# VectorE alone forms the Strassen-Winograd combinations of activations, and the second batch is transposed into two pairs of banks in turn

## The chip, the core and the metric

The kernel runs on one core of a Trainium2 chip. The time is the device time of one execution in microseconds (us), median of three runs; lower is better. TensorE multiplies 128x128 blocks and writes its results into PSUM, which has eight banks of 128 partitions x 512 fp32 elements. VectorE, ScalarE and GpSimd do the elementwise work; SyncE issues most DMAs. In the profile they are PE, DVE, ACT, POOL and SP, and PEld is TensorE's loading of weights.

## The reference

One encoder layer is applied to two batches of 512 tokens with the same weights. Only its beginning matters for the change: the normalised activations h and the wide input projection.

```python
def rms_norm(x, g):
    xf = x.astype(jnp.float32)
    y = xf * lax.rsqrt(jnp.mean(xf * xf, axis=-1, keepdims=True) + EPS) * g.astype(jnp.float32)
    return y.astype(x.dtype)

def hybrid_layer(x, norm_g, w_in, ...):
    h = rms_norm(x, norm_g)                       # (1, 512, 1024)
    proj = jnp.einsum('bsd,de->bse', h, w_in)     # w_in: 1024 x 6848
    c_q, c_kv, k_rope, gate_a, conv_in, gate_c, mg_a, mg_c = split_columns(proj)
    ...                                           # attention, convolution, merge
    u = conv_in[..., :CONV_WIDTH] * jax.nn.sigmoid(conv_in[..., CONV_WIDTH:])
    ...                                           # width-31 depthwise convolution of u, and the rest

y_prompt = hybrid_layer(x_prompt, ...)
y_sample = hybrid_layer(x_sample, ...)
```

## The kernel before

**Precision.** Every fp32 operand of a matmul is held as two rounded parts, a high part H and a low part L = value - H, and a product is three matmuls: H·H, L·H and H·L. For a weight block `i`, `split` makes `whi` (ScalarE, L128) and `wlo` (L129, VectorE for the first four blocks, GpSimd later).

**The two batches.** Batch 0 (prompt) and batch 1 (sample) have 512 tokens each, in four tiles `xt` of 128 tokens. `norm_x` squares and sums a tile on ScalarE (L263), forms the factor `rr` on VectorE and GpSimd (L264, L251) and scales the tile on VectorE (L267, L270). `trans_x` transposes it on TensorE into PSUM tiles `xT` (L275), one tile of one bank for each block k of 128 channels, k from 0 to 7. `evac_x` writes the high part `hH` (ScalarE, L306) and the low part `hL` (VectorE, L307).

**Combinations.** A part of the projection (`seven`, from about 113 us on) computes four 512-wide products with seven, after Strassen and Winograd, treating the two batches and the two halves of the channels as a 2x2 block matrix. It needs four combinations of the activations for each k from 0 to 3, each with a high and a low part, `tH` and `tL`. `whole_x` first adds `hH` and `hL` of batch 0 to `xw` on GpSimd (L284). Then `combine_x(k)` works on the banks of batch 1 for k and k + 4:

- `b22` is bank k + 4 times the gain (ScalarE, L290);
- `t1 = bank k * gain - xw[k]` and `t3 = bank k * gain - b22` (VectorE, L291 and L292);
- `t2 = b22 - t1` and `t4 = xw[k+4] - t2` (GpSimd, L293 and L294);
- for each of t1, t3, t2, t4, `tH` is a rounded copy (ScalarE, L298) and `tL = t - tH` (GpSimd, L299).

The buffers of t1 to t4 and of `b22` are single, so the next k waits until they are read.

**Banks.** At the beginning pool `pp` holds three pairs of banks and pool `p1` two single banks. Two of the pairs hold `first[0]` and `first[1]` (named `blk`), the first two projection blocks. Batch 1 is transposed into the two single banks of `p1`, for k and k + 4 together; the transposes of the next k wait until all readers of these two banks are done: `hH`, `hL`, `b22`, t1 and t3. The third pair of `pp` is free during this time.

**From the preparation to the steady part.** `block_mm` for batch 0 of the two blocks (48 matmuls) runs while batch 1 is normalised; 48 more follow for batch 1. Then both pools are closed, and six single banks `pb` take the place of `pp`. The first block after that (`pbi`, `single`) is given the two banks of `first[1]`. It may start when those have been read: ScalarE makes `sig`, the sigmoid of `first[0]` (L487, after a load of its table), and VectorE multiplies `first[1]` by it into `u` (L494), in two halves. The weights `whi` and `wlo` have three buffers each, so those of the fourth block (`split` ahead of `sig` on ScalarE and ahead of `u` on VectorE) wait until the matmuls of `first[0]` have read the first block's.

**What sets the order.** The whole program is written down in one pass; a list scheduler then places each engine's instructions in an order of its own, from dependencies and priorities, except inside the `manual_schedule` blocks. So an edit at the beginning may move instructions elsewhere as well. At run time each engine takes its instructions strictly in that order.

Of the kernel before, what the change touches and what calls it, by code (L numbers as in the profile page):

```python
# [9 lines left out]
F32 = mybir.dt.float32  # L10
# [7 lines left out]
P = 128  # L18
D = 1024
S = 512  # L20
# [23 lines left out]
def encoder_block(tc, xp_d, xs_d, win_d, wkr_d, whd_d, wqr_d, wo_d, wp_d, wout_d, vec_d, dwk_d, rg_d, rc_d, yp_d, ys_d):  # L44
    nc = tc.nc
    opened = {}

    def open_pool(name, **kw):
        if kw.get("space") is not DRAM:
            kw["reuse_waits"] = "tile"  # L50
        cm = tc.tile_pool(name=name, **kw)
        opened[name] = cm
        return cm.__enter__()
# [5 lines left out]
    f = lambda ap: ap.bitcast(F32)  # L59
    mm = nc.tensor.matmul  # L60
    ACT = nc.scalar.activation
    DVE = nc.vector
# [17 lines left out]
    pp = open_pool("pp", bufs=3, space=PSUM)  # L80
# [191 lines left out]
    def trans_x(b, banks, ks):  # L272
        for tt in range(4):
            for k in ks:
                nc.tensor.transpose(banks[k][:, tt * P : (tt + 1) * P], xt[4 * b + tt][:, k * P : (k + 1) * P], identf)  # L275

    tp = open_pool("hT", bufs=1, side="right")
    TH = {(n, k): tp.tile([P, S], F32R, name=f"tH{n}_{k}") for n in (1, 2, 3) for k in range(4)}
    TL = {(n, k): tp.tile([P, S], F32R, name=f"tL{n}_{k}") for n in (1, 2, 3) for k in range(4)}
    xw = {k: tp.tile([P, S], F32, tag=f"t4_{k}", name=f"xw{k}") for k in range(KD)}  # L280

    def whole_x(k):

        nc.gpsimd.tensor_add(xw[k], f(hH[k, 0]), f(hL[k, 0]))  # L284

    def combine_x(k, banks):
        g1, g2 = (vec[:, V_NG + q : V_NG + q + 1] for q in (k, k + 4))
        b22 = xpool.tile([P, S], F32, tag="b22", name=f"b22_{k}")
        t = {n: wp.tile([P, S], F32, tag=f"s{n}", bufs=1, name=f"t{n}_{k}") for n in (1, 2, 3, 4)}
        ACT(b22, banks[k + 4], AF.Identity, scale=g2)  # L290
        DVE.scalar_tensor_tensor(t[1], banks[k], g1, xw[k], op0=ALU.mult, op1=ALU.subtract)  # L291
        DVE.scalar_tensor_tensor(t[3], banks[k], g1, b22, op0=ALU.mult, op1=ALU.subtract)  # L292
        nc.gpsimd.tensor_sub(t[2], b22, t[1])  # L293
        nc.gpsimd.tensor_sub(t[4], xw[k + 4], t[2])  # L294
        TH[4, k] = tp.tile([P, S], F32R, tag=f"t4_{k}", name=f"tH4_{k}")
        TL[4, k] = tp.tile([P, S], F32R, tag=f"t4_{k + 4}", name=f"tL4_{k}")
        for n in (1, 3, 2, 4):
            nc.scalar.copy(TH[n, k], t[n])  # L298
            nc.gpsimd.tensor_sub(TL[n, k], t[n], f(TH[n, k]))  # L299

    def evac_x(b, banks, ks):
        for k in ks:
            g = vec[:, V_NG + k : V_NG + k + 1]
            hi = hp.tile([P, S], F32R, name=f"hH{k}_{b}")
            lo = hp.tile([P, S], F32R, name=f"hL{k}_{b}")
            ACT(hi, banks[k], AF.Identity, scale=g)  # L306
            DVE.scalar_tensor_tensor(lo, banks[k], g, f(hi), op0=ALU.mult, op1=ALU.subtract)  # L307
            hH[k, b], hL[k, b] = hi, lo

    def x_bank(b, k):  # L310
        return p1.tile([P, S], F32, tag="p1", name=f"xT{b}_{k}")
# [121 lines left out]
    banks = {}  # L433
# [18 lines left out]
        block_mm(first[i], i, hh, hl, (0,))  # L452
    for k in range(KD):
        whole_x(k)
    for k in range(4):
        banks = {kk: x_bank(1, kk) for kk in (k, k + 4)}
        trans_x(1, banks, banks)
        evac_x(1, banks, banks)
        combine_x(k, banks)
    for i in (0, 1):  # L460
        block_mm(first[i], i, hh, hl, (1,))
        ensure(3 + i)
# [119 lines left out]
    pp = open_pool("pp", bufs=3, space=PSUM)  # L582
# [373 lines left out]
    for s_ in range(4 * NU + 3):  # L956
        n, j = divmod(s_, 4)
# [46 lines left out]
    pp = open_pool("pp2", bufs=4, space=PSUM)  # L1004
# [131 lines left out]
```

## Time and profile before

| | us |
|---|---|
| time, median of 3 runs (lowest to highest) | 1182.81 (1182.19 to 1184.61) |
| the profiled execution: its time, its span | 1184.55, 1182.8 |
| TensorE busy | 1145.4 (97%) |
| VectorE, ScalarE, GpSimd busy | 763.1, 488.5, 343.3 |
| granted TensorE clock, mean | 0.99 |

The profile shows one execution. The span is the time from its first to its last instruction; the execution took 1.75 us more than its span. A row of a timeline has the start in us, the duration in us, the engine, the line, the operation, and in brackets the idle time before it with what ended it. A row of the chain has start, duration, engine, name and line. A row of the waits has who waited for whom, then the sum in us, the number of times, and the longest. A row of the windows has the stretch, its length, then busy time and count for PE, PEld, DVE, ACT and POOL, and last the granted clock (1.00 is full speed), the DMA share and GB/s.

### The profile page before, as it was taken

What the parts mean: (1) busy time and instruction counts of PE and PEld (TensorE: products, weight loads), DVE (VectorE), ACT (ScalarE), POOL (GpSimd) and SP (SyncE); (2) the same over time, 40 slices, a digit from 0 to 9 for tenths busy, and PEclk for the clock granted to TensorE, in tenths of its full rate; (3) what the DMA queues carried; (4) which work ended last, traced back from release to release, by engine and by line L of the source; (5) the groups of instructions that cost most, each with busy time, mean ns of one, the idle gap of its engine ahead of it and who ended that gap; (6) DMA issues with size and microseconds to landing.
All of it is one profiled execution on the core that took longest, in us unless ns stands there. A gap on an engine that the chain in (4) does not pass through costs nothing.

```text
span 1182.8 us, 15035 instructions
## 1 busy us (share of the span) xinstructions
PE 1145.4 (97%) x5856; PEld 969.4 (82%) x5856; DVE 763.1 (65%) x1112; ACT 488.5 (41%) x909; POOL 343.3 (29%) x292
## 2 busy tenths in 40 slices
PE   6689999999999999999999999999999999999998
PEld 4468888888888888877888887899999998888887
DVE  5589899989999962652212454787877789344311
ACT  6522344343343222871101335776676687122200
POOL 5853566586576322200000001322122221000000
PEclk9889999999999999999999999999999999999999
DMA  6011223223223444534343012101100111344431
GB/s 253 1 54 71 71 89 111 86 71 107 89 107 107 160 147 151 158 115 160 138 142 125 23 52 76 39 26 34 35 25 19 36 36 37 107 135 166 161 107 72
DMA packets 46519, 109.52 MB, mean 93 GB/s; under 512 B 3696, under 2 KB 20336, under 8 KB 46448
## 3 DMA queue, kind: packets, MB, share of 16 engines
q1 hardware_dynamic: 41552, 91.78, 23.6%
q10 hardware_dynamic: 4896, 16.78, 3.5%
q8 instruction: 46, 0.75, 0.3%
q14 instruction: 25, 0.20, 0.1%
HBM read 79.18 MB, written 29.36 MB: 92 GB/s over the span
## 4 chain that ended last, share of the span: by engine, by line
PE 92%; POOL 3%; ACT 3%; DVE 1%; issue 1%; DMA 1%; SPq 0%; ACTq 0%; DVEq 0%
PE blk L325 22%; PE pbi L325 20%; PE po L1058 7%; PE pt L825 2%; PE pbd L356 2%; PE pba L356 2%; PE pbb L356 2%; PE pbd L358 2%; PE pba L358 2%; PE pbb L358 2%; PE pbb L357 2%; PE pbd L357 2%; PE pba L357 2%; PE pkv L733 1%; PE pkv L735 1%; PE pkv L734 1%
## 5 line engine op out<-in xcount | busy, mean ns | idle before, releaser
L412 DVE SCALAR_TENSOR_TENSOR py<-u,dwk,py 128x1024 f32<-128x1024 f32 x224 | 288.5, 1288 | 6.2
L128 ACT CAST whi<-raw 128x1024 fp32r<-128x1024 f32 (+3 forms) x59 | 60.5, 1025 | 282.0 <-PE blk L325 165.8
L325 PE MATMUL pbi<-hH,whi 128*128 128x512 f32 x352 | 138.9, 395 | 8.1 <-DVE u L494 8.1
L325 PE MATMUL pbi<-hL,whi 128*128 128x512 f32 x352 | 137.9, 392 | 0.0
L325 PE MATMUL pbi<-hH,wlo 128*128 128x512 f32 x352 | 108.9, 391 | 0.0
L129 DVE TENSOR_TENSOR wlo<-raw,whi 128x1024 fp32r<-128x1024 f32 (+2 forms) x38 | 53.4, 1405 | 59.9 <-ACT whi L128 59.9
L325 PEld LDWEIGHTS pbi<-hH,whi 128*128 128x128 f32 x352 | 66.6, 189 | 22.1 <-DVE u L494 8.5
L325 PEld LDWEIGHTS pbi<-hH,wlo 128*128 128x128 f32 x352 | 66.5, 189 | 14.0
L325 PEld LDWEIGHTS pbi<-hL,whi 128*128 128x128 f32 x352 | 66.7, 190 | 13.6
L179 POOL TENSOR_TENSOR olo<-s,ohi 128x512 fp32r<-128x512 f32 x44 | 57.5, 1318 | 52.7 <-ACT ohi L178 52.7
L129 POOL TENSOR_TENSOR wlo<-raw,whi 128x1024 fp32r<-128x1024 f32 x20 | 48.4, 2418 | 83.5 <-ACT whi L128 83.5
L325 PE MATMUL blk<-a,whi 128*128 128x512 f32 x256 | 68.4, 389 | 0.0
L816 ACT ACTIVATE pr<-sc,nm,sqs 128x512 f32<-128x512 f32 x64 | 51.2, 800 | 28.3 <-DVE nm L814 28.2
L251 POOL TENSOR_TENSOR rk<-sk,mhalf 128x4 f32<-128x4 f32 x16 | 17.2, 1074 | 147.7 <-DVE sk L743 147.7
L325 PE MATMUL blk<-hH,whi 128*128 128x512 f32 x144 | 57.6, 406 | 1.2 <-ACT hH L306 0.7
L325 PE MATMUL blk<-hL,whi 128*128 128x512 f32 x144 | 57.8, 401 | 0.5 <-DVE hL L307 0.4
L178 ACT CAST ohi<-s 128x512 fp32r<-128x512 f32 x44 | 26.2, 620 | 75.2 <-PE pbi L325 51.0
L325 PEld LDWEIGHTS blk<-a,whi 128*128 128x128 f32 x256 | 48.0, 188 | 9.9
L179 POOL TENSOR_TENSOR olo<-raw,ohi 128x512 fp32r<-128x512 f32 x33 | 43.7, 1324 | 35.2 <-ACT ohi L178 26.5
L325 PE MATMUL blk<-cH,whi 128*128 128x512 f32 x128 | 50.7, 396 | 2.4 <-ACT whi L128 2.4
L1061 DVE TENSOR_TENSOR o<-po,xr 128x1024 f32<-128x1024 f32 (+1 forms) x9 | 10.0, 1106 | 64.2 <-PE po L1058 64.2
L603 DVE TENSOR_TENSOR tmc<-blk,smc 128x1024 f32<-128x1024 f32 x8 | 9.8, 1225 | 64.2 <-PE blk L325 64.2
(272 smaller groups left out, 3076.5 us busy)
## 6 DMA issues: line engine op xcount, KB each, us to landing
raw<-in_win_dram SPq DMA_DIRECT2D x53, 512.0 KB, 3.6
y_s<-y SPq DMA_DIRECT2D x8, 512.0 KB, 4.0
ga_s<-stga ACTq DMA_DIRECT2D x8, 512.0 KB, 2.6
gc_s<-stgc ACTq DMA_DIRECT2D x8, 512.0 KB, 2.6
yt<-y_s SPq DMA_DIRECT2D x8, 512.0 KB, 5.3
gt<-gc_s SPq DMA_DIRECT2D x8, 512.0 KB, 4.1
mc_s<-stmc ACTq DMA_DIRECT2D x8, 512.0 KB, 3.4
raw<-in_wp_dram SPq DMA_DIRECT2D x8, 512.0 KB, 5.1
```

The source lines that it names most:

```text
L128: nc.scalar.copy(hv, rv)
L129: (sub or DVE).tensor_sub(lv, rv, f(hv))
L178: nc.scalar.copy(hi[:, sl], src)
L179: nc.gpsimd.tensor_sub(lo[:, sl], src, f(hi[:, sl]))
L325: mm(ps[b] if isinstance(ps, list) else ps[:, b], (wlo if wl_ else whi)[:, k], xl(k, b) if xl_ else xh(k, b), start=(k == 0 and wl_ == 0 a ...
L356: mm(ps, hi[:, k], xh, start=first and k == 0, stop=False, skip_group_check=not first)
L357: mm(ps, hi[:, k], xl, start=False, stop=False, skip_group_check=not first)
L358: mm(ps, lo[:, k], xh, start=False, stop=k == 3, skip_group_check=not first)
L412: DVE.scalar_tensor_tensor(out, u[:, :, i : i + S], dwk[:, j, i : i + 1], src, op0=ALU.mult, op1=ALU.add)
L816: ACT(pr, ps, AF.Exp, bias=nm, scale=r["sq"][:, j : j + 1], accum_out=sm)
L825: nc.tensor.transpose(pt[:, kt], pr[:, kt * P : (kt + 1) * P], identf)
L1058: mm(ps[:, n], lhs[k][:, ts_], w[k][:, n * S : (n + 1) * S], start=first_, stop=last_)
```

## The change

The four kinds of subtraction that GpSimd did in `combine_x` (t2, t4 and the four `tL` of each k: 24 in all) are given to VectorE. And batch 1 is transposed into two pairs of banks in turn: k = 0 and 2 use the single banks of `p1` as before, k = 1 and 3 use the third pair of `pp`. `combine_x(k)` is written after the transposes and evacuation of k + 1. Seven lines are added, so that lines after 461 have a number that is 7 higher afterwards: `u` is L501 and `sig` is L494 there.

```diff
@@ combine_x
         ACT(b22, banks[k + 4], AF.Identity, scale=g2)
         DVE.scalar_tensor_tensor(t[1], banks[k], g1, xw[k], op0=ALU.mult, op1=ALU.subtract)
         DVE.scalar_tensor_tensor(t[3], banks[k], g1, b22, op0=ALU.mult, op1=ALU.subtract)
-        nc.gpsimd.tensor_sub(t[2], b22, t[1])
-        nc.gpsimd.tensor_sub(t[4], xw[k + 4], t[2])
+        DVE.tensor_sub(t[2], b22, t[1])
+        DVE.tensor_sub(t[4], xw[k + 4], t[2])
...
         for n in (1, 3, 2, 4):
             nc.scalar.copy(TH[n, k], t[n])
-            nc.gpsimd.tensor_sub(TL[n, k], t[n], f(TH[n, k]))
+            DVE.tensor_sub(TL[n, k], t[n], f(TH[n, k]))
@@ encoder_block
     for k in range(KD):
         whole_x(k)
-    for k in range(4):
-        banks = {kk: x_bank(1, kk) for kk in (k, k + 4)}
-        trans_x(1, banks, banks)
-        evac_x(1, banks, banks)
-        combine_x(k, banks)
+    held = {}
+    for k in range(5):
+        if k < 4:
+            if k % 2:
+                two = pp.tile([P, 2, S], F32, tag="pp", name=f"xT1_{k}")
+                held[k] = {k: two[:, 0], k + 4: two[:, 1]}
+            else:
+                held[k] = {kk: x_bank(1, kk) for kk in (k, k + 4)}
+            trans_x(1, held[k], held[k])
+            evac_x(1, held[k], held[k])
+        if k > 0:
+            combine_x(k - 1, held[k - 1])
```

What the scheduler makes of it is seen at three places. In the names the first number is k (or, for `t` and `tL`, the k of the combination), and the last one numbers the buffer.

The first place is VectorE at the end of the preparation, up to `u`. Its reading of `blk_312`, which is `first[1]`, frees two banks for `pbi`. Before:

```order
L307 SCALAR_TENSOR_TENSOR hL_1_470<-xT_3_459,vec,hH_1_469 128x512
L307 SCALAR_TENSOR_TENSOR hL_1_474<-xT_7_460,vec,hH_1_473 128x512
L291 SCALAR_TENSOR_TENSOR t_3_478<-xT_3_459,vec,xw_151 128x512
L292 SCALAR_TENSOR_TENSOR t_3_480<-xT_3_459,vec,b_3_477 128x512
L129 TENSOR_TENSOR wlo_555<-raw_552,whi_554 128x1024
L494 TENSOR_TENSOR u_583<-blk_312,sig_580 128x512 x2
L412 SCALAR_TENSOR_TENSOR py_651<-u_583,dwk,y_649 128x1024
```

And now:

```order
L307 SCALAR_TENSOR_TENSOR hL_1_452<-xT_3_438,vec,hH_1_451 128x512
L294 TENSOR_TENSOR t_2_459<-xw_154,t_2_457 128x512
L299 TENSOR_TENSOR tL_2_142<-t_2_457,tH_2_130 128x512
L291 SCALAR_TENSOR_TENSOR t_3_476<-xT_3_438,vec,xw_151 128x512
L292 SCALAR_TENSOR_TENSOR t_3_478<-xT_3_438,vec,b_3_475 128x512
L299 TENSOR_TENSOR tL_2_466<-t_2_459,tH_2_465 128x512
L293 TENSOR_TENSOR t_3_477<-b_3_475,t_3_476 128x512
L299 TENSOR_TENSOR tL_3_139<-t_3_476,tH_3_127 128x512
L299 TENSOR_TENSOR tL_3_147<-t_3_478,tH_3_135 128x512
L294 TENSOR_TENSOR t_3_479<-xw_155,t_3_477 128x512
L299 TENSOR_TENSOR tL_3_143<-t_3_477,tH_3_131 128x512
L129 TENSOR_TENSOR wlo_553<-raw_550,whi_552 128x1024
```

Behind these rows stand `u`, twice, and then the last `tL`. All but one of the 24 subtractions stand ahead of `u` on VectorE.

The second place is ScalarE at the same point of the program. Before:

```order
L298 CAST tH_3_135<-t_3_480 128x512
L128 CAST whi_554<-raw_552 128x1024
L128 CAST whi_592<-raw_590 128x1024
L298 CAST tH_2_449<-t_2_443 128x512
L298 CAST tH_3_131<-t_3_479 128x512
L487 ACT_TABLE_LOAD
L487 ACTIVATE sig_580<-blk_287 128x512 x2
```

And now:

```order
L298 CAST tH_3_135<-t_3_478 128x512
L298 CAST tH_3_131<-t_3_477 128x512
L128 CAST whi_552<-raw_550 128x1024
L494 ACT_TABLE_LOAD
L494 ACTIVATE sig_578<-blk_287 128x512 x2
L128 CAST whi_590<-raw_588 128x1024
L298 CAST tH_3_485<-t_3_479 128x512
```

The copy of the fifth block's weights (`whi_590`) and the copy of a t4 now stand behind `sig`, not ahead of it.

The third place is TensorE in the attention, far from the edit, where head 0 of batch 1 and the preparation of head 1 are interleaved (`sc` are scores, `pkr` transposed keys). Before:

```order
L787 MATMUL pkT_0_5838<-identf,ks_0_5749 128x128 x4
L794 MATMUL pkr_0_5847<-identr,kk_0_5729 128x128 x4
L809 MATMUL sc_1_2_5813<-k_1_5628,qrT_1_5572 128x512
L810 MATMUL sc_1_2_5813<-k_1_5629,qrT_1_5572 128x512
L796 MATMUL pkr_0_5848<-identr,kk_0_5729 128x128 x4
L835 MATMUL av_0_1_5861<-pt_5769,vh_0_5295 128x256
```

And now:

```order
L794 MATMUL pkT_0_5836<-identf,ks_0_5747 128x128 x4
L816 MATMUL sc_1_2_5811<-k_1_5626,qrT_1_5570 128x512
L817 MATMUL sc_1_2_5811<-k_1_5627,qrT_1_5570 128x512
L801 MATMUL pkr_0_5845<-identr,kk_0_5727 128x128 x4
L803 MATMUL pkr_0_5846<-identr,kk_0_5727 128x128 x4
L842 MATMUL av_0_1_5859<-pt_5767,vh_0_5293 128x256
```

Two matmuls of the scores moved ahead of four transposes. Elsewhere after the beginning TensorE's order is unchanged; on VectorE some steps of the convolution (L412) change places with their neighbours by one or a few, ScalarE and GpSimd have a few such exchanges, and SyncE has one.

## The prediction

> **What bounds the kernel now.** I read the page first (part 1, then the chain that ended last), then TensorE's waits, the chain in order of time at the beginning, and the timeline there.
>
> ```profile
> PE 1145.4 (97%) x5856; PEld 969.4 (82%) x5856; DVE 763.1 (65%) x1112; ACT 488.5 (41%) x909; POOL 343.3 (29%) x292
> PE 92%; POOL 3%; ACT 3%; DVE 1%; issue 1%; DMA 1%; SPq 0%; ACTq 0%; DVEq 0%
> PE pbi L325 <- DVE u L494: 8.1, 1, 8.1
> PE xT L275 <- ACT b L290: 4.6, 3, 2.5
> PE pkr L796 <- ACT k L798: 1.9, 1, 1.9
> ```
>
> TensorE is the bound, and a change elsewhere pays only where TensorE waits. Its longest wait after the start is one of 8.1 us, of the first block `pbi` for `u`; the next, 4.6 us in three parts, is of the second batch's transposes for `b22`. The change is aimed at both. In the attention no wait is longer than 1.9 us. The chain shows what stands behind the first two:
>
> ```profile
> 32.00 0.75 DVE hL L307
> 34.14 1.27 POOL tL L299
> 42.95 1.23 POOL t L293
> 47.56 7.87 PE blk L325 x24
> 55.45 1.06 ACT whi L128
> 56.84 5.28 issue
> 63.55 1.29 DVE u L494 x2
> 64.88 7.27 PE pbi L325 x22
> ```
>
> From 34 us on the chain goes through GpSimd, then TensorE, then 5.28 us that it cannot explain ("issue"). The timeline does:
>
> ```profile
> 55.45 2.18 ACT L128 CAST whi<-raw 128x1024 fp32r<-128x1024 f32 x2 [1.21 <-PE blk L325]
> 56.54 7.09 DVE L129 TENSOR_TENSOR wlo<-raw,whi 128x1024 fp32r<-128x1024 f32 x1 [2.96 <-ACT whi L128]
> 59.06 0.62 ACT L298 CAST tH<-t 128x512 fp32r<-128x512 f32 x1 [0.91 <-POOL t L293]
> 59.70 1.28 ACT L487 ACT_TABLE_LOAD   x1
> 60.99 1.09 ACT L487 ACTIVATE sig<-blk 128x512 f32<-128x512 f32 x2
> 64.88 0.80 PE L325 MATMUL pbi<-hH,whi 128*128 128x512 f32 x1 [8.11 <-DVE u L494]
> 533.50 1.22 DVE L129 TENSOR_TENSOR wlo<-raw,whi 128x1024 fp32r<-128x1024 f32 x1 [4.58 <-ACT whi L128]
> 34.14:66.00 31.86, 18.73 (x69) 12.97 (x70) 17.86 (x16) 19.41 (x30) 31.77 (x30) 0.78 0.03 10
> ```
>
> Two things delay `u`. ScalarE's queue waits for GpSimd's `t` (0.91 us, ahead of the table and `sig`, which ends at 62.08). And VectorE's `wlo`, which takes 1.22 us at 533.50, takes 7.09 us here, to 63.6, while GpSimd is busy without a gap: 31.77 of the 31.86 us from 34.14 on (last row, fifth pair). So `sig` alone would have let `u` begin at 62.1; the slow `wlo` costs 1.4 us more.
>
> [...]
>
> **The new list on VectorE.** GpSimd loses 24 subtractions, VectorE gains them; 23 stand ahead of `u`. With GpSimd out of the way the list can be priced from undisturbed rows.
>
> ```profile
> 32.67 0.74 DVE L291 SCALAR_TENSOR_TENSOR t<-xT,vec,xw 128x512 f32<-128x512 f32 x1
> 33.33 0.74 DVE L307 SCALAR_TENSOR_TENSOR hL<-xT,vec,hH 128x512 fp32r<-128x512 f32 x1
> 658.50 1.89 DVE L645 TENSOR_TENSOR kvL<-kvn,kvH 128x512 fp32r<-128x512 f32 x3
> 662.10 0.68 DVE L645 TENSOR_TENSOR kvL<-kvn,kvH 128x512 fp32r<-128x512 f32 x1
> L298 ACT CAST tH<-t 128x512 fp32r<-128x512 f32 x15 | 9.0, 616 | 7.7 <-POOL t L293 6.1 <-DVE t L291 0.9 <-DVE t L292 0.7
> ```
>
> Three-operand instructions follow each other 0.67 us apart (32.00, 32.67, 33.33). A subtraction of the kind of `tL` takes 0.68 alone and three take 1.89, so they stand 0.605 apart; `wlo` then takes about 1.14 from its neighbour. From the first `hL` of batch 1 at 32.00 to `u` the order has 16 of the first (8 `hL`, 4 t1, 4 t3), 23 of the second and one `wlo`: 10.7 + 13.9 + 1.1 = 25.7, so `u` could start at 57.7. Its two halves take 1.29: `pbi` could start at 59.0. ScalarE has 15 casts of 0.62 where it had 15 before and keeps up.
>
> - ScalarE's chain to `sig`: the t2 of k = 3 is the 35th in the list (16 three-operand ones, 19 subtractions), done at 32.0 + 22.2 + 0.1 = 54.3; its cast to 54.9; `whi` 1.06, the table 1.28, `sig` 1.09: 58.3. The second half of `u` then ends at 59.0 as well. Both lists meet.
> - TensorE can be later. `whi` needs the buffer of the first block's weights, so nearly all of `first[0]` and `first[1]`. The `hL` of k = 3 is the 24th in VectorE's list (13 and 11), done at 47.4; 28 matmuls remain, 6.4 us at the 0.227 us spacing below: 53.8, hidden under 54.9. At half clock they take longer, by 1.7 us (one 3.4 us stretch) to 3.4 us (two): 55.5 to 57.2. `whi` starts some 0.5 before the last, so between 54.9 and 56.7, and `pbi` 4.1 us later (1.06 + 1.28 + 1.09 + 0.68).
>
> So `pbi` starts between 59.0 and 60.9. I take 60.2, near the upper end, since the next rows show the clock at half speed in just this part. Against 64.88 that is 4.7 us earlier (4.0 to 5.9).
>
> ```profile
> 38.45:41.85 3.40, 2.09 (x11) 1.25 (x12) 1.50 (x2) 2.65 (x5) 3.40 (x4) 1.00 0.01 2
> 41.85:45.25 3.40, 1.09 (x4) 0.55 (x4) 1.50 (x2) 1.19 (x3) 3.40 (x3) 1.00 0.00 0
> 45.25:48.65 3.40, 3.06 (x11) 2.24 (x12) 1.51 (x3) 2.98 (x6) 3.40 (x4) 0.50 0.01 2
> 48.65:52.05 3.40, 3.40 (x10) 2.63 (x9) 1.19 (x2) 0.46 (x1) 3.40 (x4) 0.50 0.00 0
> 52.05:55.45 3.40, 3.40 (x16) 2.80 (x15) 1.05 (x2) 1.88 (x4) 3.40 (x4) 1.00 0.00 0
> 55.45:58.85 3.40, 1.32 (x6) 0.75 (x4) 2.31 (x1) 2.62 (x3) 3.40 (x3) 1.00 0.00 0
> 65.65:69.05 3.40, 3.40 (x10) 2.66 (x9) 2.79 (x3) 1.01 (x2) 0.94 (x2) 0.50 0.63 259
> 69.05:72.45 3.40, 3.40 (x17) 2.79 (x16) 3.33 (x3) 0.00 (x0) 3.40 (x4) 0.99 0.00 0
> 1004.63 87.07 PE blk L325 x384
> ```
>
> **The clock.** I chose stretches of 3.4 us because the clock changes at their edges. It fell to 0.50 after stretches with 1.09 and 1.32 us of TensorE work, not after 2.09; it rose after the full ones from 48.65 and from 65.65, not after 3.06. At full speed 384 matmuls take 87.07 us, 0.227 each; the half-speed stretches hold 10 where a full one holds 15 or more. After 64.88 half speed lasts to 69.05, 4.2 us, and costs half of it, 2.1 us. In the new kernel the gap ahead of `pbi` is still some 4 us, so the clock falls again. Half speed then lasts from one full stretch to nearly two, 3.4 to 6.8 us, by where `pbi` falls in them: 1.7 to 3.4 us, I take 2.6. That is 0.5 more than now (-0.4 to +1.3).
>
> [...]
>
> **The second pair of banks.** The 4.6 us of waits for `b22` go: k = 1 has its own banks, and its transposes follow those of k = 0. But the next matmuls then wait for `hL`, which stands in VectorE's longer list. These waits are inside the 47.4 above; I count no gain of their own. If VectorE's list were short they would be worth up to 4.6.
>
> **What moves otherwise.** The six small fills of `u`, the fifth block's `wlo` and the sums stay on GpSimd; between the factors `rr` and `sig` it has nothing but the fills. The convolution on VectorE starts earlier with `u`, one `tL` behind; TensorE waits for nothing until the attention. There the exchange of scores and transposes can only lose, since TensorE has no gap at that place now:
>
> ```profile
> 755.00:766.00 11.00, 11.00 (x83) 10.15 (x83) 7.79 (x24) 9.22 (x23) 3.90 (x4) 1.00 0.01 1
> ```
>
> The loss lies between 0 and 1.9 us, the longest wait of the attention; I take 0.3, as the queues there have most of their inputs ready.
>
> **Sum.** -4.7 + 0.5 + 0.3 = -3.9 us. The profiled execution took 1184.55 us with a span of 1182.8, so it would take 1180.6. It lies 1.74 above the median of the runs; for the median 1182.8 - 3.9 = 1178.9 us, 0.33% less.
>
> **Rivals.**
>
> - *The clock holds over the shorter gap.* If both stretches that share the gap keep more than about 1.5 us of work, there is no fall, and the 2.1 us go too: -4.7 - 2.1 + 0.3 = -6.5, 1176.3 us. For it: the gap shrinks from 8.1 to 4; against it: a gap of 2.5 us was enough at 45.25.
> - *The gain is lost again.* The worst ends of TensorE's part (`pbi` at 60.9), the clock (+1.3) and the attention (+1.9) leave -4.0 + 3.2 = -0.8: 1182.0, no change that can be told; 2.4 us, 0.2% of the time, is about what this measurement can tell from none. For it: VectorE has no slack left, so each late cast delays everything behind it.
> - *Slower: VectorE and GpSimd still collide.* The undisturbed price holds only while GpSimd is quiet:
>
> ```profile
> 15.10 11.99 POOL L284 TENSOR_TENSOR xw<-hH,hL 128x512 f32<-128x512 f32 x8 [3.33 <-DVE hL L307]
> 23.70 2.24 DVE L129 TENSOR_TENSOR wlo<-raw,whi 128x1024 fp32r<-128x1024 f32 x1
> ```
>
> While GpSimd adds up `xw`, a `wlo` takes 2.24, 1.0 more than alone, so half as wide a subtraction 0.5 more. For 23 of them that is 11.5 us, and the time becomes 1178.9 + 11.5 = 1190.4. It decides from 0.17 us per subtraction on (3.9 / 23). Against it: the order gives GpSimd no such work in this stretch.
>
> **Chances.** Forecast (VectorE's list, `pbi` at 59 to 60.9, clock falls again) 0.62; clock holds 0.13; gain lost 0.20; collision 0.05. The forecast's own range is 1177 to 1181.2; a tenth of it lies above 1180.4. So faster 0.62 x 0.92 + 0.13 = 0.70, same 0.25, slower 0.05. The range with both sides, less than 2 in 10 left out, is 1175.6 to 1181.9.
>
> **What would show it.** Right: VectorE without a gap from 32 to 59, subtractions at 0.6 to 0.7 us, `wlo` of the fourth block at 1.2, the wait of `pbi` at 3 to 5 us and its start near 60; no wait for `b22`, waits for `hL` instead. Wrong: subtractions over 0.8 us, a clock of 1.00 after `pbi`'s start, or a new wait between 740 and 770 us. The forecast fails most easily by the clock, whose stretches need not fall at the same places in another execution.

## The result, and the profile after

In the first comparison the changed kernel takes 1176.55 us (median of 4 runs, 1173.73 to 1177.61), the kernel before 1183.35 (1182.19 to 1184.61). The ratio is 0.9939, 95% interval 0.9917 to 0.9960: 6.8 us less. The profiled execution took 1175.7 us, its span is 1173.9, 8.9 less than the 1182.8 before. The same kernel was compared twice more later (e8, e10 below): 1180.53 against 1184.04 (0.9963, 0.9949 to 0.9977) and 1179.87 against 1183.84 (0.9967, 0.9955 to 0.9979). There it gains 3.5 and 4.0 us. The forecast was 3.9. One execution of e5 below, at 1642.49 us with a granted clock of 0.65, is left out of its median.

First the busy times of the changed kernel and TensorE's waits from 31 to 72 us (who waited for whom; sum, times, longest):

```profile
PE 1139.5 (97%) x5856; PEld 965.2 (82%) x5856; DVE 774.7 (66%) x1136; ACT 488.9 (42%) x909; POOL 312.6 (27%) x268
PE pbi L325 <- DVE u L501: 3.7, 1, 3.7
PE blk L325 <- DVE hL L307: 3.3, 3, 1.8
PE blk L325 <- ACT hH L306: 2.7, 3, 1.9
PE xT L275 <- DVE t L292: 1.5, 1, 1.5
```

The wait of `pbi` went from 8.1 to 3.7, the 4.6 us for `b22` are gone, and 7.5 us of waits for `hL`, `hH` and t3 stand in their place (before: 0.9 for `hH` and t3). Then the chain in order of time (start, duration, engine, name, line) and three rows of VectorE:

```profile
31.00 0.75 DVE hL L307
45.62 0.67 DVE hL L307
46.33 8.55 PE blk L325 x25
54.91 0.25 ACT whi L128
55.97 1.28 ACT L494
59.24 12.97 PE pbi L325 x50
...
55.98 1.23 DVE L129 TENSOR_TENSOR wlo<-raw,whi 128x1024 fp32r<-128x1024 f32 x1 [0.51 <-ACT whi L128]
57.89 1.29 DVE L501 TENSOR_TENSOR u<-blk,sig 128x512 f32<-128x512 f32 x2 [0.69 <-ACT sig L494]
59.83 2.45 DVE L299 TENSOR_TENSOR tL<-t,tH 128x512 fp32r<-128x512 f32 x1 [0.65 <-ACT tH L298]
```

GpSimd has left the chain from 31 us on; VectorE's list stands in it up to the `hL` of k = 3, then 25 matmuls, `whi`, the table (55.97), `sig` and `u`. The `wlo` takes 1.23 us instead of 7.09. From the first `hL` to `pbi` it is 59.24 - 31.00 = 28.24 us, before 64.88 - 32.00 = 32.88: 4.64 less.

That is half of the 8.9. The clock accounts for most of the rest. Windows of the changed kernel (fifth column group is GpSimd; then the granted clock), and of the same two places of the program further on, before and after:

```profile
55.25:58.65 3.40, 0.30 (x2) 0.00 (x0) 2.20 (x4) 3.37 (x5) 0.00 (x0) 1.00 0.13 24
58.65:62.05 3.40, 2.81 (x7) 2.23 (x8) 2.75 (x2) 2.29 (x3) 2.38 (x1) 0.51 0.35 130
527.30:530.30 3.00, 2.93 (x12) 2.09 (x13) 1.20 (x1) 0.00 (x0) 0.00 (x0) 1.00 0.92 333
726.80:730.80 4.00, 4.00 (x31) 3.75 (x30) 1.84 (x5) 3.17 (x8) 0.00 (x0) 1.00 0.31 120
```

```profile
533.50:536.50 3.00, 2.98 (x7) 2.43 (x8) 1.22 (x1) 0.00 (x0) 0.00 (x0) 0.50 0.93 306
734.20:738.20 4.00, 4.00 (x21) 3.83 (x20) 1.50 (x4) 2.88 (x6) 0.00 (x0) 0.57 0.31 119
```

The second fence is the kernel before. There the clock fell behind the wait for `whi` (at 533) and again in the attention (at 734); in the changed kernel's first profile it fell at neither place. The last part is the start: ScalarE's squares of the third input row, which wait for that row to land, begin at 7.64 us instead of 8.33, in a part that the change doesn't touch, and the first `hL` of batch 1 came 1.0 us earlier. Comparing the start of the same blocks in both traces, the 8.9 us are: start 1.0, from `hL` to `pbi` 4.6, half speed after `pbi` 0.7 (2.8 us of it instead of 4.2), the fall at 533 1.1, the fall at 734 1.5.

### The profile page after: what moved, and what is told of

It is laid out like the page before. It is cut to its first block, busy times and chain, and to the rows that moved or that the text cites. A ratio compares the mean times of both kernels' runs of the same rounds, so it can differ in the third digit from the quotient of the medians.

```text
span 1173.9 us, 15039 instructions
## 1 busy us (share of the span) xinstructions
PE 1139.5 (97%) x5856; PEld 965.2 (82%) x5856; DVE 774.7 (66%) x1136; ACT 488.9 (42%) x909; POOL 312.6 (27%) x268
## 3 DMA queue, kind: packets, MB, share of 16 engines
q1 hardware_dynamic: 41552, 91.78, 23.9%
## 4 chain that ended last, share of the span: by engine, by line
PE 92%; DVE 3%; ACT 2%; POOL 2%; issue 1%; DMA 0%; SPq 0%; ACTq 0%; DVEq 0%
PE blk L325 22%; PE pbi L325 21%; PE po L1065 7%; PE pt L832 2%; PE pbd L358 2%; PE pba L358 2%; PE pbb L358 2%; PE pbd L357 2%; PE pba L357 2%; PE pbb L357 2%; PE pbd L356 2%; PE pba L356 2%; PE pbb L356 2%; PE pkv L740 1%; PE pkv L742 1%; PE pkv L741 1%
## 5 line engine op out<-in xcount | busy, mean ns | idle before, releaser
L412 DVE SCALAR_TENSOR_TENSOR py<-u,dwk,py 128x1024 f32<-128x1024 f32 x224 | 288.5, 1288 | 6.3
L129 DVE TENSOR_TENSOR wlo<-raw,whi 128x1024 fp32r<-128x1024 f32 (+2 forms) x38 | 47.6, 1252 | 58.0 <-ACT whi L128 58.0
```

The source lines that it names most:

```text
L129: (sub or DVE).tensor_sub(lv, rv, f(hv))
L412: DVE.scalar_tensor_tensor(out, u[:, :, i : i + S], dwk[:, j, i : i + 1], src, op0=ALU.mult, op1=ALU.add)
```

## The experiments

The first question is what made the 4.6 us, the second how much of the 6.8 belongs to the change, the third what bounds this part now. "hL to pbi" is the time from the first `hL` of batch 1 to `pbi`; it does not depend on the start or on what the clock does further on.

| kernel | hL to pbi, us | median, us | ratio to before (95%) |
|---|---|---|---|
| before | 32.88 | 1183.35 to 1184.04 | 1 |
| changed, first | 28.24 | 1176.55 | 0.9939 (0.9917 to 0.9960) |
| e8, changed | 28.18 | 1180.53 | 0.9963 (0.9949 to 0.9977) |
| e10, changed | 27.75 | 1179.87 | 0.9967 (0.9955 to 0.9979) |
| e1, subtractions alone | 29.10 | 1181.01 | 0.9973 (0.9963 to 0.9983) |
| e2, banks alone | 36.89 | 1187.17 | 1.0027 (1.0016 to 1.0038) |
| e7, GpSimd kept busy | 39.03 | 1190.78 | 1.0057 (1.0042 to 1.0072) |
| e4, gap filled | 27.94 | 1176.34 | 0.9940 (0.9924 to 0.9957) |
| e11, gap filled | 28.58 | 1176.82 | 0.9941 (0.9928 to 0.9954) |
| e5, TensorE's order | 27.97 | 1180.26 | 0.9966 (0.9952 to 0.9979) |
| e3, `sig` and `u` first | 25.87 | 1173.46 | 0.9908 (0.9895 to 0.9922) |
| e9, subtractions behind `u` | 19.50 | 1170.42 | 0.9884 (0.9870 to 0.9897) |
| e12, e9 again | 19.49 | 1170.30 | 0.9882 (0.9868 to 0.9895) |
| e13, e12 with the gap filled | 19.50 | 1168.80 | 0.9872 (0.9859 to 0.9886) |

e1, e2, e4 and e7 were compared together; so were e3, e5, e8 and e9; and e10 to e13.

**The two halves of the change (e1, e2).** e1 is the kernel before with the subtractions on VectorE:

```diff
-        nc.gpsimd.tensor_sub(t[2], b22, t[1])
-        nc.gpsimd.tensor_sub(t[4], xw[k + 4], t[2])
+        DVE.tensor_sub(t[2], b22, t[1])
+        DVE.tensor_sub(t[4], xw[k + 4], t[2])
...
-            nc.gpsimd.tensor_sub(TL[n, k], t[n], f(TH[n, k]))
+            DVE.tensor_sub(TL[n, k], t[n], f(TH[n, k]))
```

> The 24 subtractions go to VectorE, the transposes of batch 1 keep the one pair of banks. Theory (the gain comes from the subtractions): from the first hL of batch 1 to the first pbi it takes 29 us (28.5 to 30.5; 28.2 in the changed kernel, 32.9 before), the fourth wlo takes 1.2 us, and the time is 1177 to 1180. Rival (the second pair of banks makes the gain): TensorE's waits for the banks stay, pbi stands at 32 us or more after the first hL, and the time is 1182 or more.

e2 is the changed kernel with these lines as before, so that only the banks change.

> Two pairs of banks in turn, the 24 subtractions stay on GpSimd. Theory (the gain comes from the subtractions): TensorE ends its blk matmuls earlier than before, but ScalarE's sig still waits behind a copy of GpSimd's t (59.1 before), so pbi stands 31 to 32.5 us after the first hL and the time is 1180 to 1183. Rival (the banks make the gain): 28 to 29 us and 1176 to 1178.

Rows of e1 (TensorE's waits, the timeline):

```profile
PE xT L275 <- ACT b L290: 5.0, 3, 2.6
31.39 0.75 DVE L307 SCALAR_TENSOR_TENSOR hL<-xT,vec,hH 128x512 fp32r<-128x512 f32 x1 [1.14 <-ACT hH L306]
60.49 0.50 PE L325 MATMUL pbi<-hH,whi 128*128 128x512 f32 x1 [3.69 <-DVE u L494]
```

and of e2, VectorE, ScalarE, GpSimd and TensorE in order of time:

```profile
49.73 9.03 DVE L129 TENSOR_TENSOR wlo<-raw,whi 128x1024 fp32r<-128x1024 f32 x1 [3.38 <-ACT whi L128]
56.41 1.27 POOL L299 TENSOR_TENSOR tL<-t,tH 128x512 fp32r<-128x512 f32 x1
58.68 0.74 DVE L291 SCALAR_TENSOR_TENSOR t<-xT,vec,xw 128x512 f32<-128x512 f32 x1
65.11 0.62 ACT L298 CAST tH<-t 128x512 fp32r<-128x512 f32 x1 [3.86 <-POOL t L293]
69.02 0.80 PE L325 MATMUL pbi<-hH,whi 128*128 128x512 f32 x1 [19.72 <-DVE u L501]
```

e1 keeps the waits for `b22` (5.0 us) and still brings `pbi` to 29.10, as the theory had it; its time is 1.0 above the range given. In time e1 can't be told from the changed kernel of the later comparisons: the intervals of the ratios overlap. The banks alone make the kernel slower, against both theories, and the rows say how. TensorE ends its blocks at 49.3, six us earlier than in the changed kernel, and so `whi` is done and `wlo` starts earlier too. The `wlo` now falls into GpSimd's run of subtractions and takes 9.03 us. Behind it in VectorE's queue stands the t1 of k = 3 (58.68), on which GpSimd's last t2 depends, and `sig` stands behind the copy of that t2 (65.11). So the banks are worth 0.9 us with the subtractions moved (29.10 against 28.24) and cost 4.0 without (36.89 against 32.88).

**The collision (e7).** The changed kernel, with 20 adds on GpSimd while VectorE works on its list:

```diff
+    spare = xpool.tile([P, D], F32, tag="junk", name="spare")
+    for r in range(20):
+        nc.gpsimd.tensor_add(spare[:, (r % 2) * S : (r % 2 + 1) * S], xt[7][:, 0:S], xt[7][:, S:D])
     held = {}
```

> The changed kernel with 20 additional adds of two 128x512 halves on GpSimd, while VectorE works on its list (from the last factor on, 1.27 us each, 25 us); nobody reads their result. Theory (the two engines collide where both read two operands from SBUF, as the 7.1 us wlo before): the 23 subtractions take 0.2 to 0.7 us more each, pbi starts 5 to 16 us later and the time is 1181 to 1192. Rival (no collision; the slow wlo had another cause): subtractions stay at 0.6 us and the time at 1176.5.

Groups of VectorE's instructions from 30 to 72 us (count, busy, mean ns of one): first three of the changed kernel, then the same of e7, then GpSimd's adds:

```profile
L299 DVE TENSOR_TENSOR tL<-t,tH 128x512 fp32r<-128x512 f32 x16 | 12.5, 800 | 0.7 <-ACT tH L298 0.7
L292 DVE SCALAR_TENSOR_TENSOR t<-xT,vec,b 128x512 f32<-128x512 f32 x4 | 3.0, 749 | 0.0
L293 DVE TENSOR_TENSOR t<-b,t 128x512 f32<-128x512 f32 x4 | 2.8, 690 | 0.0
```

```profile
L299 DVE TENSOR_TENSOR tL<-t,tH 128x512 fp32r<-128x512 f32 x16 | 19.9, 1260 | 0.6 <-ACT tH L298 0.6
L293 DVE TENSOR_TENSOR t<-b,t 128x512 f32<-128x512 f32 x4 | 5.3, 1327 | 0.0
L292 DVE SCALAR_TENSOR_TENSOR t<-xT,vec,b 128x512 f32<-128x512 f32 x4 | 2.9, 737 | 0.0
L457 POOL TENSOR_TENSOR spare<-xt 128x512 f32<-128x512 f32 x20 | 31.5, 1611 | 0.9 <-DVE xt L270 0.9
```

The subtractions take 1.26 and 1.33 us instead of 0.69 to 0.80 (the mean of L299 in the changed kernel holds one of 2.45 us behind `u`), though GpSimd's adds cover at most 31.5 of the 39.0 us up to `pbi`; the adds take 1.61. The instructions that read one operand from a bank (t3, L292) take no longer, 0.74 us against 0.75. The time is 1190.78, `pbi` 10.8 us later. So VectorE's list is as short as it is only because GpSimd is quiet beside it: 28.24 us from the first `hL` to `pbi`, against 39.03 here.

**The same kernel again (e8, e10).** Unaltered.

> The changed kernel once more, unaltered, for how far two profiled executions of the same program differ. Theory: VectorE's list from the first hL of batch 1 to pbi takes 28.2 us again (28.0 to 28.5), and what differs are the first hL's start (31 or 32 us, by when the third input row lands) and the places further on where the clock falls (none in the first profile, near 530 and 740 in others), 0 to 3 us together. Rival (the change makes the clock hold further on): no fall after 100 us again, and the time is 1176.5.

> The changed kernel unaltered, a third time, beside the next three. Theory (28.2 us from the first hL to pbi each time; the start and the clock's falls after pbi, near 530 and near 740 differ from execution to execution): 28.2 us again, and a time of 1174 to 1181.

Rows of e8: the first `hL`, `pbi`, and windows around `pbi` and at the two places further on; then the window after `pbi` of e10.

```profile
32.55 0.75 DVE L307 SCALAR_TENSOR_TENSOR hL<-xT,vec,hH 128x512 fp32r<-128x512 f32 x1 [1.14 <-ACT hH L306]
60.73 0.80 PE L325 MATMUL pbi<-hH,whi 128*128 128x512 f32 x1 [3.69 <-DVE u L501]
60.06:63.47 3.41, 2.75 (x7) 2.17 (x8) 2.76 (x3) 2.37 (x3) 2.38 (x1) 0.50 0.37 137
63.47:66.88 3.41, 3.41 (x10) 2.64 (x9) 3.34 (x4) 0.00 (x0) 0.01 (x1) 0.50 0.46 154
531.40:534.70 3.30, 3.30 (x9) 2.54 (x9) 0.09 (x1) 0.00 (x0) 0.00 (x0) 0.53 0.88 314
743.00:746.90 3.90, 3.90 (x19) 3.45 (x18) 3.33 (x9) 3.00 (x7) 1.05 (x1) 0.60 0.01 2
```

```profile
59.71:65.40 5.69, 5.69 (x13) 4.46 (x14) 5.02 (x4) 1.70 (x3) 2.38 (x1) 0.50 0.46 150
```

From `hL` to `pbi` it is 28.18 and 27.75 us again. But half speed lasts 6.2 (to 66.9) and 5.7 us after `pbi` instead of 2.8, and the clock falls twice further on, as it did before the change: near 530 behind the same wait for `whi`, and in the attention, there some 11 us further on in the program than before (in e10 it is 0.50 from 530.0 to 533.0 and from 741.5 to 744.6). With as many falls on both sides the profiled executions differ by 3.0 us (1179.8 against 1182.8: start +0.55, `hL` to `pbi` -4.7, half speed after `pbi` +1.0, the rest +0.15) and 4.5 us (1178.3: about 0, -5.1, +0.7, -0.1). That is the size of the later comparisons.

**The clock ahead of `pbi` (e4, e11).** The changed kernel with matmuls in the gap, whose result nobody reads:

```diff
     with tc.manual_schedule(engines={nc.tensor.engine}):
+        fill = py.tile([P, 2, S], F32, tag="py", name="fill")
+        for _ in range(12):
+            mm(fill[:, 0], identr, TL[2, 3], start=True, stop=True)
```

> The changed kernel with 12 additional matmuls of 128x512 whose result nobody reads, between the last blk matmul and the first pbi; they start when the last tL of k = 3's t2 is there (55.4) and take 2.7 us. Theory (the clock falls because of the gap, and half speed costs 1.4 us): the clock is 1.00 after pbi's start, pbi starts at the same place (28.2 us after the first hL), its second to seventh matmul follow at 0.23 us instead of 0.43, and the time is 1.4 us shorter, about 1175.2. Rival (the clock goes by something other than TensorE's work in a stretch): it falls again, and the time is that of the changed kernel, 1176.5.

> The changed kernel with the 12 additional matmuls in the gap ahead of pbi (e4), now beside the changed kernel on the same chip. Theory (the fall of the clock ahead of pbi costs 1.4 us where half speed lasts 2.8 us after pbi's start, 2.9 where it lasts 5.8): full clock after pbi's start, and 1.4 to 2.9 us less than the changed kernel in the same comparison. Rival (a fall that is kept off here comes further on instead, or none is saved): within 1 us of it.

`pbi` and the window behind it, of e11:

```profile
62.28 0.50 PE L325 MATMUL pbi<-hH,whi 128*128 128x512 f32 x1 [0.93 <-DVE u L501]
62.28:66.00 3.72, 3.72 (x16) 3.11 (x17) 3.13 (x2) 1.70 (x3) 2.41 (x1) 1.00 0.24 86
```

The clock stays at 1.00 (in e4 too, from `pbi` at 59.94 to 65). e4 read as a miss against the first comparison's 1176.55 (no gain); beside the changed kernel, e11 gains 3.05 us (1176.82 against 1179.87, and the intervals of the ratios just part), where 5.7 us at half speed would cost 2.9. The two profiled executions alone would not show it: e11's is hardly shorter than e10's (spans 1178.2 and 1178.3), since its first `hL` came 1.7 us later and `hL` to `pbi` took 0.8 us longer. The rival of a fall put off is excluded for this place; the falls near 530 and 741 happen in e11 as in e10.

**What bounds this part now (e5, e3, e9, e12, e13).** The edit of e5 changes TensorE's order alone:

```diff
-        block_mm(first[i], i, hh, hl, (1,))
+        block_mm(first[i], i, hh, hl, (1,), ks=(0, 4, 1, 5, 2, 6, 3, 7))
```

> The changed kernel with the blk matmuls of batch 1 in the order k = 0, 4, 1, 5, 2, 6, 3, 7 in which their operands come, instead of 0 to 7. Theory (TensorE stands 1.8 us for the hL of k = 3 with matmuls of k = 4 to 6 ready behind it): blk ends by 52 instead of 55.5, but then VectorE's list (55.4) and ScalarE's last t2 (53.7) hold pbi, so it gains 1.2 us only, 27.0 after the first hL, and 1175.3. Rival (TensorE's order sets pbi): 3 us or more, 1173.5 or less.

e3 leaves that as it was and puts `sig` and `u` ahead of the fourth block's weights, with the table loaded beforehand:

```diff
+    warm = xpool.tile([P, D], F32, tag="junk", name="warm")
+    ACT(warm[:, 0:1], mhalf[:, 0:1], AF.Sigmoid)
     first = {}
...
-    for nm, i in (("cb", 0), ("ca", 1)):
-        take(nm, 0, [first[i][:, b] for b in range(2)])
+    with tc.manual_schedule(engines={nc.scalar.engine, nc.vector.engine}):
+        for nm, i in (("cb", 0), ("ca", 1)):
+            take(nm, 0, [first[i][:, b] for b in range(2)])
+        ensure(4, 0)
```

> The changed kernel with sig and u ahead of the fourth block's whi and wlo on ScalarE and VectorE, and the table of the sigmoid loaded earlier, at 26 us. Theory (after VectorE's list ends at 55.4, pbi waits only for whi, the table and wlo, one behind the other): u starts right behind the list, at 55.5 to 55.8, pbi 26.0 us after the first hL instead of 28.2, and the time is 2.1 us shorter, or 3.5 where the clock holds over the shorter gap: 1173 to 1174.5. Rival (u is bound by the list or by the fourth block anyway): pbi moves by less than 0.5 us and the time stays at 1176.5.

The copy of the last t2 and `pbi` in e5, then `u` and `pbi` in e3:

```profile
55.48 0.62 ACT L298 CAST tH<-t 128x512 fp32r<-128x512 f32 x1 [1.42 <-DVE t L293]
59.38 0.80 PE L325 MATMUL pbi<-hH,whi 128*128 128x512 f32 x1 [10.79 <-DVE u L501]
```

```profile
56.42 1.29 DVE L504 TENSOR_TENSOR u<-blk,sig 128x512 f32<-128x512 f32 x2
57.77 0.50 PE L325 MATMUL pbi<-hH,whi 128*128 128x512 f32 x1 [1.56 <-DVE u L504]
```

In e5 TensorE is done 10.8 us before `pbi`, and the time hardly changes: 1180.26 against 1180.53 for e8, less than the 1.2 us expected. The trace shows what took its place. `wlo` now stands in VectorE's list ahead of the last t2 (at 50.26), and one `tL` behind it took 1.53 us, where its neighbour took 0.69; so the copy of that t2, behind which the table and `sig` stand, ends 24.7 us after the first `hL` instead of 22.7 (changed kernel). TensorE's end and VectorE's list bind nearly together, and e5 alone doesn't price the first. In e3 `u` starts with no idle time ahead of it, so VectorE's list is what it now waits for; `pbi` comes 2.3 us earlier than in e8, as expected, the clock stays at 1.00 after it (to 63.0), and by the mean granted clock (0.996, in e8 0.991) there was no fall further on either, which is why 7.1 us came out against e8, and not 2.1 to 3.5. The missing falls further on are luck, as in the first comparison.

e9 takes both edits, gives t1, t2, t3 and `b22` more buffers, and moves 16 subtractions behind `u`. The core of it:

```diff
+        for k in range(4):
...
+            comb_a(k, held[k])
+            if k > 0:
+                comb_t2(k - 1)
+                comb_l(1, k - 1)
+        comb_t2(3)
...
+            take(nm, 0, [first[i][:, b] for b in range(2)])
+        ensure(4, 0)
+        for k in range(4):
+            for n in (2, 3) if k < 3 else (1, 2, 3):
+                comb_l(n, k)
+            comb_4b(k, comb_4(k))
```

`comb_a` makes `hH`, `hL`, `b22`, t1 and t3 of one k, `comb_t2` the t2, `comb_l(n, k)` the `tH` and `tL`, and `comb_4` with `comb_4b` the t4 with its `tH` and `tL`.

> The changed kernel with three things: the matmuls in the order of e5, sig and u ahead of the fourth block's weights as in e3, and 16 of the 23 subtractions behind u on VectorE instead of ahead of it (t1, t2, t3 keep buffers of their own, so that no k waits for another). Theory (VectorE's list ahead of u sets pbi): 16 three-operand instructions and 7 subtractions stand ahead of u, 15 us, so pbi comes 16.5 to 18 us after the first hL instead of 28.2, and the clock has no cause to fall: 10 to 12 us less, 1164.5 to 1167. Rival (the convolution on VectorE, busy without a gap from 62 us on, bounds the part that follows): the work put behind u is paid there, and the time is 1172 to 1176.

> The kernel of e9 (subtractions behind u, sig ahead of the weights, matmuls in the order of their operands) once more. Theory: 19.5 us from the first hL to pbi again, 8.7 less than in the changed kernel, and 8 to 11 us less in time. Rival (the 10 us of the first comparison were luck with the clock): 8 us or less.

```profile
46.08 0.75 DVE L299 SCALAR_TENSOR_TENSOR t<-xT,vec,xw 128x512 f32<-128x512 f32 x1 [0.76 <-ACT b L298]
52.05 0.50 PE L347 MATMUL pbi<-hH,whi 128*128 128x512 f32 x1 [2.47 <-DVE u L528]
53.30:56.60 3.30, 3.30 (x9) 2.53 (x9) 3.30 (x3) 1.00 (x1) 2.07 (x1) 0.51 0.63 179
```

Above are rows of e9: one of VectorE's gaps, `pbi`, and the window behind it. It takes 19.50 us from the first `hL` (32.55) to `pbi`, e12 19.49: 8.7 less than in the changed kernel, though 1.5 to 3 more than expected, since VectorE now has four gaps of 0.76 us in which it waits for `b22` or `hH` of ScalarE (first row). Against the changed kernel in the same comparison the time is 10.1 (1170.42, 1180.53) and 9.6 us less (1170.30, 1179.87), within the 10 to 12 and the 8 to 11 expected; the absolute range of e9, reckoned from 1176.55, was missed by 3 us for the reason that e8 shows. The rival is refuted: the work put behind `u` is not paid in the convolution.

The clock still fell, 1.1 us after `pbi` (the last row begins just behind the fall). e13 adds 9 matmuls to the gap of e9:

```diff
     with tc.manual_schedule(engines={nc.tensor.engine}):
+        fill = py.tile([P, 2, S], F32, tag="py", name="fill")
+        for _ in range(9):
+            mm(fill[:, 0], identr, hL[7, 1], start=True, stop=True)
```

> The kernel of e9 with 9 additional matmuls (2.0 us) in its gap of 2.5 us ahead of pbi; nobody reads their result. Theory (the gap is what let the clock fall 1.3 us after pbi's start in e9, at 53.4 to 56.7 us): no fall there, pbi at the same place, and 1.6 us less than e9 in the same comparison. Rival (a gap of 2.5 us does not matter, the fall is of another cause): a fall there again, and the same time.

```profile
51.50 0.50 PE L347 MATMUL pbi<-hH,whi 128*128 128x512 f32 x1 [0.40 <-DVE u L528]
51.50:57.00 5.50, 5.50 (x24) 4.53 (x25) 5.50 (x5) 3.92 (x7) 4.99 (x1) 1.00 0.33 95
```

No fall there, `pbi` at 19.50 again, and 1.5 us less than e12 (1168.80, 1170.30). The intervals of the two ratios overlap, and e13's profile also lacks the fall that e12's has at 519, so the time alone does not show it; the clock in the window does. e13 is the fastest kernel here, 1.28% below the kernel before (1.14 to 1.41).

## Why the prediction was right, point by point

The forecast was 1178.9, 3.9 us less. The three comparisons gave 6.8, 3.5 and 4.0 less, all inside its range. By its own steps:

- **VectorE's list: right.** No gap up to the last `tL` at 55.5, subtractions 0.60 apart, `wlo` 1.23. The `hL` of k = 3 was to end 15.4 us after the first; it ended at 46.28, 15.3 after. `pbi` was to come 4.7 us earlier: 4.64, 4.70 and 5.13, counted from the first `hL`. e1 shows the subtractions alone to be worth 3.8 of it (32.88 to 29.10), and e7 that a quiet GpSimd is the condition.
- **TensorE is a little later than the list: right, and within the stated times.** The last 25 matmuls, the first of them at half speed, took 8.55 us; `whi` began at 54.91, 23.9 after the first `hL`, where 22.9 to 24.7 was the range, and the table, `sig` and `u` followed one behind the other. That VectorE's list would meet it there was right as well: in e5, with TensorE out of the way, the list holds `pbi` at nearly the same place.
- **The clock: right in kind, its size from 1.4 to 3.1.** It fell ahead of `pbi` in all three profiles. 2.6 us was taken; half speed lasted 2.8 us in the first profile (cost 1.4), 6.2 and 5.7 in the next two (3.1 and 2.9). e11 gives the price as a time, between medians: 3.05 us. The range 3.4 to 6.8 for the length was too high at its lower end. In the first comparison the term was thus -0.7 instead of +0.5.
- **What the sum left out: the clock further on.** It had TensorE wait for nothing from `pbi` to the attention. That is a misreading: in the kernel before TensorE waits 2.45 us for `whi` near 530 (row below), and the clock falls behind this wait. The profile of before holds a second fall in the attention; the two are worth 1.1 and 1.5 us, and the prediction names neither. In the first profile of the changed kernel they are missing, in the next two they are back. With the start (1.0) they make the difference between 8.9 and 4.6 + 0.7; the change itself does none of the three by what these runs show, since the same program has them and has them not. That the first comparison exceeded the forecast by 2.9 us is thus luck.
- **The second pair of banks: no gain of their own was nearly right.** 0.9 us with the subtractions moved, and a loss of 4.0 without, which the prediction did not see: it called the waits for `b22` worth up to 4.6 if VectorE's list were short. In e2 VectorE's list is short, and the waits are indeed gone, but TensorE only reaches its next wait earlier.
- **The attention: 0 instead of +0.3.** Its waits are the same in both (1.9 for `k` is the longest).
- **The rivals.** The collision did not come ahead of `u`, and its price was right: 1190.4 was said, e7 with GpSimd busy gave 1190.78. The clock did not hold over the gap in any profile of the changed kernel; where it was made to hold, in e11, it was worth 3.05, where the prediction's two sums are 2.6 apart (6.5 and 3.9). The gain was not lost.

The wait that the prediction passed over, in the kernel before:

```profile
533.51 0.80 PE L325 MATMUL blk<-cH,whi 128*128 128x512 f32 x1 [2.45 <-ACT whi L128]
```

In e10 half speed begins at 41.5, ends at 51.7, begins at 58.6 and ends at 65.4: three stretches of 3.41 us and then two, with two at full speed between them. With the same program the clock falls near 530 in e8 and e10, and not in the first profile. As to the gap, 2.45 us was enough in e12, where the clock fell 0.5 us after `pbi`; in e13, with 9 matmuls (2.23 us) in a gap of the same size, the clock did not fall.

## What to carry to other kernels

When an instruction is moved from one engine's queue to another, look at what stands behind the late one in that queue: here `sig` and `u` waited not for their inputs but for copies and subtractions that are needed 50 us later, and putting those behind `u`, together with the two smaller edits of e9 (2.3 us for `sig` and `u` first, in e3), was worth more (8.7 us) than the change itself (4.6). A shorter wait upstream can lose if it makes an instruction start beside an engine that it collides with (in e2 `wlo` took 9.03 us beside GpSimd, in the changed kernel 1.23, and `pbi` came 4.0 us later than in the kernel before). And a gain of half a per cent needs the clock of both profiles along the whole span, and the same kernel more than once, before the time is read.

## What the runs showed of the hardware

All of this is read from the traces of this case; what inside the chip brings it about, they do not tell.

**A wide subtraction on VectorE waited for a pause of GpSimd.** Rows of GpSimd in the kernel before, where VectorE's `wlo` ran from 56.54 to 63.63, and of the changed kernel:

```profile
61.28 1.26 POOL L299 TENSOR_TENSOR tL<-t,tH 128x512 fp32r<-128x512 f32 x1
62.49 0.12 POOL L490 MEMSET u<- 128x30 f32 x1
```

```profile
59.36 2.38 POOL L129 TENSOR_TENSOR wlo<-raw,whi 128x1024 fp32r<-128x1024 f32 x1 [17.32 <-ACT whi L128]
```

In the kernel before, `wlo` ended 1.1 us after GpSimd's last subtraction in the run gave way to fills (62.49 + 1.14 = 63.63). In e2 GpSimd's run ended at 57.68 and `wlo` at 58.76, 1.1 after. In the changed kernel GpSimd's own `wlo` ended at 61.74, and VectorE's `tL` of 2.45 us at 62.28, 0.5 after. Undisturbed, `wlo` takes 1.22 us (at 533.50 in the kernel before) and `tL` 0.69; so each seems to have waited for the end of what GpSimd was doing and then to have taken about its usual time, and in the kernel before and in e2 the wide one did not get in between several GpSimd instructions that followed each other. In e7 the half as wide subtractions did get in between GpSimd's adds: from 30.65 to 62.10 GpSimd is busy for all of the 31.45 us and VectorE for 30.46, the groups of subtractions take 1.16 to 1.33 us on average, and the adds became longer (1.61, where the adds to `xw` in the kernel before have a median of 1.29). The width alone does not make the difference: in the kernel before, the `wlo` at 23.70, just as wide, took 2.24 us beside GpSimd's adds (the row is in the prediction), which fits a wait for one of them, and the two adds beside this `wlo` and the one ahead of it took 2.27 us, the others 1.29. What makes the difference was not tried.

**In these profiles the clock changed on a grid of 3.41 us, and near 530 a fall went with the place of a wait in it.** In the kernel before, the changed kernel's first profile, e9, e10, e11, e12 and e13, and in e5 from 475 us on, all changes of the clock lie whole multiples of 3.413 us apart (in the kernel before, from 69.14 to 533.36, it is 136 times 3.413). The wait for `whi` near 530 has about the same length in both kernels, 2.45 us before and 2.4 after. Here are the steps of the grid that hold it, in the changed kernel's first profile, where it spreads over two steps, and in e8, where it lies in one:

```profile
522.90:526.31 3.41, 1.95 (x9) 1.29 (x7) 0.00 (x0) 1.20 (x3) 0.00 (x0) 1.00 0.25 68
526.31:529.72 3.41, 2.36 (x9) 1.65 (x10) 1.23 (x1) 0.93 (x1) 0.00 (x0) 1.00 0.98 374
527.69:531.11 3.42, 0.97 (x5) 0.67 (x4) 0.84 (x1) 2.09 (x3) 0.00 (x0) 1.00 0.82 254
```

In e8 TensorE works for only 0.97 us of that step, and behind it the clock is at 0.50. At this wait nine profiles agree: seven have a step with little work and a fall behind it (e8 0.97 us; the kernel before 1.12; e5, e9, e10, e11 and e12 between 0.96 and 1.41), and two have at least 1.9 us in each step and no fall (the changed kernel's first, above; e13). In the attention busy time is not the measure: the fall of e10 at 741.24 follows a step with 2.4 us of work or more, that of the kernel before at 734.74 one with 1.54.

**When half speed ended was not told by TensorE's busy time.** Full speed came back after a stretch with 2.81 us of work in 3.40 (first profile of the changed kernel, 58.65 on), and not after one with 2.75 in e8 (60.06 on) nor after the one with 3.06 of the kernel before (45.25 on). What decides it stays open.
